# Two groups of 64 rows in place of 65 and 63, and third and fourth pieces stored 16 rows at a time

## The chip, the cores and the metric

The kernel runs on one core of a Trainium2 chip. The metric is device time in microseconds, the median of several executions; the profile is of one further execution. "Span" is the time from the first to the last instruction of that execution.

## What is computed

For each of 16 x 1024 tokens the two largest of 8 router logits are found, the softmax over those two gives two weights, and the token's vector of 512 numbers is written twice, once times each weight (the lower weight first).

```python
batch, seq, hidden, n_experts, k = 16, 1024, 512, 8, 2
topk_indices = np.argsort(probs, axis=-1)[..., -k:]
topk_probs = np.take_along_axis(probs, topk_indices, axis=-1)
topk_probs = topk_probs / np.sum(topk_probs, axis=-1, keepdims=True)
x_expanded = x[:, :, np.newaxis, :].repeat(k, axis=2)
return (x_expanded * topk_probs[..., np.newaxis]).astype(np.float32)
```

All is float32. 33.6 MB of x and 0.5 MB of logits are read, 67.1 MB are written.

## The kernel before

The 16,384 tokens are split over 128 partitions. Every partition has 128 tokens, here called rows: a row of x is 2 KB in a partition, a row of the output 4 KB. The rows are worked on in two groups, of 65 and then 63 rows in a partition (`GROUPS`, line 49). A partition's rows of one group are contiguous in DRAM, so that in the output the blocks of neighbouring partitions begin 260 KB apart in group 0 and 252 KB apart in group 1, and in x 130 and 126 KB.

SBUF holds three tiles: `logits`; `xs`, 65 rows of x (line 95); and `osp`, 16 rows of output (line 96). There is too little room for a group's whole output, which is twice its input, so most of the output is written over rows of x that have been used: `over(r, n, G)` (lines 98 to 104) gives the part of `xs` where the output of rows r to r + n goes.

Group by group, in program order:

1. `LOADS` (lines 51, 111 and 112) loads x in pieces, on SP's queue: 2, 4, 2, 8, 17 and 32 rows in group 0, 16, 16 and 31 in group 1. After the first 6 rows the logits are loaded too (lines 116 and 117), and `top2_weights` computes all weights at once: eleven small VectorE operations and two sigmoids on ScalarE, with a tile for each intermediate result.
2. `plan` (lines 120 to 126) lists the pieces of output. In group 0: rows 0 and 1 into `osp`; rows 2 to 15 into `osp`; rows 16 to 31 over `xs` rows 0 to 31; rows 32 to 39 and 40 to 47 into the two halves of `osp`; rows 48 to 56 over `xs` rows 31 to 48, rows 57 to 64 over 49 to 64. In group 1 rows 0 to 15 are one piece, and the last is rows 48 to 62 (`LAST`, line 54).
3. For each piece VectorE makes one multiply (line 128), then the piece is stored (line 136), on SP's queue except the first piece of 2 rows, which goes on ScalarE's.

Each engine's queue runs in program order. A multiply into `osp` waits for the store that last read that part of `osp`; one over `xs` waits for a store that still reads that part of `xs`. A load of group 1 waits until the stores that read its part of `xs` have landed, and it stands behind all stores of group 0 in SP's queue. The stores of group 1 stand behind its loads.

Of the kernel before, what the change touches and what calls it, by code (L numbers as in the profile page):

```python
# [1 line left out]

# [4 lines left out]

F32 = mybir.dt.float32
ALU = mybir.AluOpType
ACTF = mybir.ActivationFunctionType  # L10
P = 128


def top2_weights(nc, pool, logits, M, E, tag=""):

    hi, lo, n = None, None, E  # L20
    while n > 1:
        n //= 2
        if hi is None:
            a, b = logits[:, :, 0:n], logits[:, :, n : 2 * n]
            nhi = pool.tile([P, M, n], F32, tag=f"hi{n}{tag}")
            nlo = b
            nc.vector.tensor_tensor(nhi, a, b, op=ALU.max)  # L27
            nc.vector.tensor_tensor(nlo, a, b, op=ALU.min)  # L28
        else:
            a, b = hi[:, :, 0:n], hi[:, :, n : 2 * n]  # L30
            nhi = pool.tile([P, M, n], F32, tag=f"hi{n}{tag}")
            nlo = pool.tile([P, M, n], F32, tag=f"lo{n}{tag}")
            tmp = pool.tile([P, M, n], F32, tag=f"tmp{n}{tag}")
            nc.vector.tensor_tensor(tmp, lo[:, :, 0:n], lo[:, :, n : 2 * n], op=ALU.max)  # L34
            nc.vector.tensor_tensor(nlo, a, b, op=ALU.min)  # L35
            nc.vector.tensor_tensor(nlo, nlo, tmp, op=ALU.max)  # L36
            nc.vector.tensor_tensor(nhi, a, b, op=ALU.max)  # L37
        hi, lo = nhi, nlo
    dlt = pool.tile([P, M], F32, tag=f"dlt{tag}")
    nc.vector.tensor_tensor(dlt, hi[:, :, 0], lo[:, :, 0], op=ALU.subtract)  # L40
    WA = pool.tile([P, M, 2], F32, tag=f"WA{tag}")
    nc.scalar.activation(WA[:, :, 0], dlt, ACTF.Sigmoid, scale=-1.0)  # L42
    nc.scalar.activation(WA[:, :, 1], dlt, ACTF.Sigmoid, scale=1.0)  # L43
    return WA

GROUPS = [65, 63]

LOADS = [[2, 4, 2, 8, 17, 32], [16, 16, 31]]


LAST = [[(48, 9), (57, 8)], [(48, 15)]]


@with_exitstack
def kernel(
    ctx: ExitStack,
    tc: tile.TileContext,  # L60
    x: bass.AP,
    router_logits: bass.AP,
    k: bass.AP,
    out: bass.AP,
):
    nc = tc.nc
    B, S, D = x.shape
    E = router_logits.shape[-1]
    N = B * S
    assert int(k) == 2 and E == 8 and N == P * sum(GROUPS)  # L70
    M = N // P

    L = 16
    x_v, o_v, rl_v = [], [], []
    t0 = 0
    for n in GROUPS:
        t1 = t0 + P * n
        x_v.append(
            x.rearrange("b s d -> (b s) d")[t0:t1].rearrange("(p m) d -> p m d", p=P)
        )  # L80
        o_v.append(
            out.rearrange("b s k d -> (b s) k d")[t0:t1].rearrange(
                "(p m) k d -> p m k d", p=P
            )
        )
        rl_v.append(
            router_logits.rearrange("b s e -> (b s) e")[t0:t1].rearrange(
                "(p m) e -> p m e", p=P
            )
        )  # L90
        t0 = t1

    wpool = ctx.enter_context(tc.tile_pool(name="wpool", bufs=1))
    logits = wpool.tile([P, M, E], F32)
    xs = wpool.tile([P, max(GROUPS), D], F32)
    osp = wpool.tile([P, L, 2, D], F32)

    def over(r, n, G):

        a = 2 * r - G
        return xs[:, a : a + 2 * n, :].rearrange("p (r k) d -> p r k d", k=2)

    h = L // 2
    e = 2
    m0 = 0
    for g, G in enumerate(GROUPS):
        r = 0  # L110
        for n in LOADS[g]:
            nc.sync.dma_start(xs[:, r : r + n, :], x_v[g][:, r : r + n, :])  # L112
            r += n
            if g == 0 and r == 6:

                nc.sync.dma_start(logits[:, :G], rl_v[0])  # L116
                nc.sync.dma_start(logits[:, G:], rl_v[1])
                WA = top2_weights(nc, wpool, logits, M, E)
        assert r == G
        begin = [(0, e, osp[:, :e]), (e, L - e, osp[:, e:])] if g == 0 else [(0, L, osp)]  # L120
        plan = begin + [
            (L, L, over(L, L, 2 * L)),
            (2 * L, h, osp[:, :h]),
            (2 * L + h, h, osp[:, h:]),
        ]
        plan += [(r, n, over(r, n, G)) for r, n in LAST[g]]
        for r, n, og in plan:
            nc.vector.tensor_tensor(  # L128
                og,
                xs[:, r : r + n, :].unsqueeze(2).to_broadcast([P, n, 2, D]),  # L130
                WA[:, m0 + r : m0 + r + n, :].unsqueeze(3).to_broadcast([P, n, 2, D]),
                op=ALU.mult,
            )

            queue = nc.scalar if n == e else nc.sync
            queue.dma_start(o_v[g][:, r : r + n], og)  # L136
        m0 += G


# [1 line left out]
_INS = ['x', 'router_logits', 'k']  # L141
_OUTS = [((16, 1024, 2, 512), 'float32')]

_NUMBERS = {'k': 2}


# [26 lines left out]
```

## Time and profile before

| | |
|---|---|
| median of 3 runs | 240.18 us (240.18 to 240.59) |
| the profiled execution's own time | 240.25 us |
| its span | 238.5 us |
| VectorE multiplies into osp | 7, 69.1 us |
| VectorE multiplies over xs | 5, 69.1 us |
| idle time before multiplies into osp | 61.9 us |
| DMA packets | 3312, 101.19 MB, mean 424 GB/s |

The time of a run is 1.8 us longer than the span, for what lies around it. SP's queue has 22 transfers (9 loads of x, 2 of logits, 11 stores), ScalarE's one store. The profile gives for every group of DMA issues the time from issue to landing, so issue plus that time is the moment at which a transfer has landed.

### The profile page before, as it was taken

What the parts mean: (1) busy time and instruction counts of PE and PEld (TensorE: products, weight loads), DVE (VectorE), ACT (ScalarE), POOL (GpSimd) and SP (SyncE); (2) the same over time, 40 slices, a digit from 0 to 9 for tenths busy, and PEclk for the clock granted to TensorE, in tenths of its full rate; (3) what the DMA queues carried; (4) which work ended last, traced back from release to release, by engine and by line L of the source; (5) the groups of instructions that cost most, each with busy time, mean ns of one, the idle gap of its engine ahead of it and who ended that gap; (6) DMA issues with size and microseconds to landing.
All of it is one profiled execution on the core that took longest, in us unless ns stands there. A gap on an engine that the chain in (4) does not pass through costs nothing.

```text
span 238.5 us, 116 instructions
## 1 busy us (share of the span) xinstructions
DVE 142.0 (60%) x23; ACT 1.8 (1%) x3; POOL 0.2 (0%) x4
## 2 busy tenths in 40 slices
DVE  0599999900299699900000699999006999990000
ACT  2000000000000000000000000000000000000000
POOL 0000000000000000000000000000000000000000
DMA  7999989899898999999999999998999989999994
GB/s 261 434 470 411 459 383 528 330 462 462 352 506 352 440 440 440 440 414 465 440 429 434 412 478 458 394 495 374 462 418 429 451 363 429 440 440 429 495 453 206
DMA packets 3312, 101.19 MB, mean 424 GB/s; under 512 B 368, under 2 KB 496, under 8 KB 880
## 3 DMA queue, kind: packets, MB, share of 16 engines
q1 hardware_dynamic: 3168, 100.14, 97.8%
q10 hardware_dynamic: 144, 1.05, 1.0%
HBM read 34.08 MB, written 67.11 MB: 424 GB/s over the span
## 4 chain that ended last, share of the span: by engine, by line
DMA 43%; DVE 41%; issue 4%; SPq 1%; ACT 0%; DVEq 0%
DVE xs L128 22%; DVE osp L128 18%; DMA out_dram<-xs 15%; DMA xs<-in_x_dram 13%; DMA out_dram<-osp 13%; DMA logits<-in_router_logits_dram 3%; SPq L112 0%; DVE nhi L27 0%; DVE logits L28 0%; DVE nlo L36 0%; DVE nhi L37 0%; DVE tmp L34 0%; DVE nlo L35 0%; SPq L116 0%; SPq L136 0%
## 5 line engine op out<-in xcount | busy, mean ns | idle before, releaser
L128 DVE TENSOR_TENSOR osp<-xs,WA 128x8192 f32<-128x8192 f32 (+3 forms) x7 | 69.1, 9908 | 61.9 <-DMA xs<-in_x_dram 31.2
L128 DVE TENSOR_TENSOR xs<-xs,WA 128x16384 f32<-128x16384 f32 (+3 forms) x5 | 69.1, 13812 | 2.2 <-DMA out_dram<-xs 2.0
L27 DVE TENSOR_TENSOR nhi<-logits 128x512 f32<-128x512 f32 x1 | 0.7, 691 | 8.3 <-DMA logits<-in_router_logits_dram 8.3
L42 ACT ACT_TABLE_LOAD x1 | 1.3, 1283 | 0.7 <-PEq L154 0.7
L28 DVE TENSOR_TENSOR logits<-logits 128x512 f32<-128x512 f32 x1 | 0.7, 692 | 0.0
L37 DVE TENSOR_TENSOR nhi<-nhi 128x256 f32<-128x256 f32 (+1 forms) x2 | 0.7, 351 | 0.0
L35 DVE TENSOR_TENSOR nlo<-nhi 128x256 f32<-128x256 f32 (+1 forms) x2 | 0.7, 350 | 0.0
L36 DVE TENSOR_TENSOR nlo<-nlo,tmp 128x256 f32<-128x256 f32 (+1 forms) x2 | 0.7, 350 | 0.0
L34 DVE TENSOR_TENSOR tmp<-logits 128x256 f32<-128x256 f32 x1 | 0.4, 418 | 0.0
L42 ACT ACTIVATE WA<-dlt 128x128 f32<-128x128 f32 x1 | 0.3, 315 | 10.2 <-DVE dlt L40 10.2
L40 DVE TENSOR_TENSOR dlt<-nhi,nlo 128x128 f32<-128x128 f32 x1 | 0.3, 291 | 0.0
L43 ACT ACTIVATE WA<-dlt 128x128 f32<-128x128 f32 x1 | 0.3, 297 | 0.0
L34 DVE TENSOR_TENSOR tmp<-nlo 128x128 f32<-128x128 f32 x1 | 0.3, 283 | 0.0
L154 POOL MEMSET const-bfloat16-1.0<- 128x1 bf16 x1 | 0.1, 101 | 0.0
L154 POOL MEMSET const-uint8-127<- 128x1 uint8 x1 | 0.1, 101 | 0.0
L154 POOL MEMSET const-float32-0.0<- 128x1 f32 x1 | 0.1, 98 | 0.2 <-issue 0.2
L154 POOL MEMSET const-float32-1.0<- 128x1 f32 x1 | 0.1, 98 | 0.0
## 6 DMA issues: line engine op xcount, KB each, us to landing
out_dram<-osp SPq DMA_DIRECT2D x4, 4096.0 KB, 20.7
xs<-in_x_dram SPq DMA_DIRECT2D x2, 4096.0 KB, 29.9
xs<-in_x_dram SPq DMA_DIRECT2D x1, 7936.0 KB, 38.0
out_dram<-xs SPq DMA_DIRECT2D x1, 7680.0 KB, 23.2
out_dram<-osp SPq DMA_DIRECT2D x1, 7168.0 KB, 33.9
out_dram<-xs SPq DMA_DIRECT2D x1, 4608.0 KB, 20.4
xs<-in_x_dram SPq DMA_DIRECT2D x1, 4352.0 KB, 22.4
out_dram<-xs SPq DMA_DIRECT2D x1, 4096.0 KB, 21.5
```

Source lines behind the costliest of these rows:

```text
L27: nc.vector.tensor_tensor(nhi, a, b, op=ALU.max)
L28: nc.vector.tensor_tensor(nlo, a, b, op=ALU.min)
L34: nc.vector.tensor_tensor(tmp, lo[:, :, 0:n], lo[:, :, n : 2 * n], op=ALU.max)
L35: nc.vector.tensor_tensor(nlo, a, b, op=ALU.min)
L36: nc.vector.tensor_tensor(nlo, nlo, tmp, op=ALU.max)
L37: nc.vector.tensor_tensor(nhi, a, b, op=ALU.max)
L40: nc.vector.tensor_tensor(dlt, hi[:, :, 0], lo[:, :, 0], op=ALU.subtract)
L42: nc.scalar.activation(WA[:, :, 0], dlt, ACTF.Sigmoid, scale=-1.0)
L43: nc.scalar.activation(WA[:, :, 1], dlt, ACTF.Sigmoid, scale=1.0)
L128: nc.vector.tensor_tensor(og, xs[:, r : r + n, :].unsqueeze(2).to_broadcast([P, n, 2, D]), WA[:, m0 + r : m0 + r + n, :].unsqueeze(3).to_b ...
L154: nc = _bacc.Bacc("TRN2", target_bir_lowering=False, num_devices=1)
```

## The change

Both groups have 64 rows. In DRAM a partition's block is then 256 KB of output and 128 KB of x in both groups.

`osp` has 18 rows in place of 16. The two more rows (`osp[:, 16:18]`) first hold all intermediate results of `top2_weights`, which had tiles of their own.

The pieces of a group are now written out. The first two (three in group 0) are as before. The third piece, rows 32 to 47, is multiplied in two parts: rows 46 and 47 first, into the two more rows of `osp`, and then rows 32 to 45 into `osp[:, 2:16]`; then one store takes all 16 rows from `osp[:, 2:18]`. The fourth piece, rows 48 to 63, is multiplied in two halves over `xs` rows 32 to 47 and 48 to 63 (`pairs`), and one store takes all 16. The pieces of 17 and 31 rows in `LOADS` become 16 and 32. Group 0 has 5 stores in place of 7 and group 1 has 4 in place of 5.

```diff
-GROUPS = [65, 63]
+GROUPS = [64, 64]
-LOADS = [[2, 4, 2, 8, 17, 32], [16, 16, 31]]
+LOADS = [[2, 4, 2, 8, 16, 32], [16, 16, 32]]
-LAST = [[(48, 9), (57, 8)], [(48, 15)]]
...
-    L = 16
+    L, e = 16, 2
...
-    osp = wpool.tile([P, L, 2, D], F32)
+    osp = wpool.tile([P, L + e, 2, D], F32)
-    def over(r, n, G):
-        a = 2 * r - G
+    def pairs(a, n):
         return xs[:, a : a + 2 * n, :].rearrange("p (r k) d -> p r k d", k=2)
...
+    def multiply(og, m0, r, n):
+        nc.vector.tensor_tensor(
+            og,
+            xs[:, r : r + n, :].unsqueeze(2).to_broadcast([P, n, 2, D]),
+            WA[:, m0 + r : m0 + r + n, :].unsqueeze(3).to_broadcast([P, n, 2, D]),
+            op=ALU.mult,
+        )
...
+                spare = osp[:, L:].rearrange("p r k d -> p (r k d)")
+                WA = top2_weights(nc, wpool, logits, spare, M, E)
...
+        if g == 0:
+            multiply(osp[:, :e], m0, 0, e)
+            nc.scalar.dma_start(o_v[g][:, :e], osp[:, :e])
+            multiply(osp[:, e:L], m0, e, L - e)
+            nc.sync.dma_start(o_v[g][:, e:L], osp[:, e:L])
+        else:
+            multiply(osp[:, :L], m0, 0, L)
+            nc.sync.dma_start(o_v[g][:, :L], osp[:, :L])
+
+        multiply(pairs(0, L), m0, L, L)
+        nc.sync.dma_start(o_v[g][:, L : 2 * L], pairs(0, L))
+
+        multiply(osp[:, L:], m0, 3 * L - e, e)
+        multiply(osp[:, e:L], m0, 2 * L, L - e)
+        nc.sync.dma_start(o_v[g][:, 2 * L : 3 * L], osp[:, e:])
+
+        multiply(pairs(2 * L, L // 2), m0, 3 * L, L // 2)
+        multiply(pairs(3 * L, L // 2), m0, 3 * L + L // 2, L // 2)
+        nc.sync.dma_start(o_v[g][:, 3 * L :], pairs(2 * L, L))
```

In `top2_weights` the tiles of the intermediate results are taken from that spare part one after another (`part(n)`); its operations and their order are the same.

More of the change, by code (lines that the diff above doesn't have):

```diff
@@ L11, with top2_weights, part @@
 P = 128
-def top2_weights(nc, pool, logits, M, E, tag=""):
+def top2_weights(nc, pool, logits, scratch, M, E):
+    at = 0
+    def part(n):
+        nonlocal at
+        at += M * n
+        return scratch[:, at - M * n : at].rearrange("p (m n) -> p m n", n=n)
     hi, lo, n = None, None, E
@@ L22, in top2_weights @@
         n //= 2
+        nhi = part(n)
         if hi is None:
             a, b = logits[:, :, 0:n], logits[:, :, n : 2 * n]
-            nhi = pool.tile([P, M, n], F32, tag=f"hi{n}{tag}")
             nlo = b
@@ L30, in top2_weights @@
             a, b = hi[:, :, 0:n], hi[:, :, n : 2 * n]
-            nhi = pool.tile([P, M, n], F32, tag=f"hi{n}{tag}")
-            nlo = pool.tile([P, M, n], F32, tag=f"lo{n}{tag}")
-            tmp = pool.tile([P, M, n], F32, tag=f"tmp{n}{tag}")
+            nlo, tmp = part(n), part(n)
             nc.vector.tensor_tensor(tmp, lo[:, :, 0:n], lo[:, :, n : 2 * n], op=ALU.max)
@@ L38, in top2_weights @@
         hi, lo = nhi, nlo
-    dlt = pool.tile([P, M], F32, tag=f"dlt{tag}")
+    dlt = part(1)[:, :, 0]
     nc.vector.tensor_tensor(dlt, hi[:, :, 0], lo[:, :, 0], op=ALU.subtract)
-    WA = pool.tile([P, M, 2], F32, tag=f"WA{tag}")
+    WA = pool.tile([P, M, 2], F32)
     nc.scalar.activation(WA[:, :, 0], dlt, ACTF.Sigmoid, scale=-1.0)
@@ L95 @@
     xs = wpool.tile([P, max(GROUPS), D], F32)
-    osp = wpool.tile([P, L, 2, D], F32)
-    def over(r, n, G):
-        a = 2 * r - G
+    osp = wpool.tile([P, L + e, 2, D], F32)
+    def pairs(a, n):
         return xs[:, a : a + 2 * n, :].rearrange("p (r k) d -> p r k d", k=2)
-    h = L // 2
-    e = 2
+    def multiply(og, m0, r, n):
[5 more added lines that the diff above has]
+        )
     m0 = 0
@@ L117 @@
                 nc.sync.dma_start(logits[:, G:], rl_v[1])
-                WA = top2_weights(nc, wpool, logits, M, E)
+                spare = osp[:, L:].rearrange("p r k d -> p (r k d)")
+                WA = top2_weights(nc, wpool, logits, spare, M, E)
         assert r == G
[L120 to L136, printed above, removed]
+        if g == 0:
[14 more added lines that the diff above has]
+        nc.sync.dma_start(o_v[g][:, 3 * L :], pairs(2 * L, L))
         m0 += G
```

## The prediction

> **What bounds the kernel now.** I read the totals and the rows of the DMA queues first, then the waits, then the timeline with the time to landing of the single stores.
>
> ```profile
> span 238.5 us, 116 instructions
> DVE 142.0 (60%) x23; ACT 1.8 (1%) x3; POOL 0.2 (0%) x4
> q1 hardware_dynamic: 3168, 100.14, 97.8%
> q10 hardware_dynamic: 144, 1.05, 1.0%
> HBM read 34.08 MB, written 67.11 MB: 424 GB/s over the span
> ```
>
> VectorE works 60% of the time. The packets of the two DMA queues (q1 is SP's, q10 ScalarE's) fill 98.8% of what 16 DMA engines have in the span. So the path that sets the end is the DMA engines' own work, and what VectorE waits for matters only if it leaves them without a transfer. Whether it does is seen by setting each transfer's issue beside the landing of the transfer ahead of it. For the last stores:
>
> ```profile
> 180.91 17.29 DVE L128 TENSOR_TENSOR osp<-xs,WA 128x8192 f32<-128x8192 f32 x2 [13.39 <-DMA out_dram<-osp]
> 189.63 8.93 SPq L136 DMA_DIRECT2D out_dram<-osp  x2
> 198.24 16.16 DVE L128 TENSOR_TENSOR xs<-xs,WA 128x15360 f32<-128x15360 f32 x1
> 214.42 0.33 SPq L136 DMA_DIRECT2D out_dram<-xs  x1
> ```
>
> The answers for the windows in which 150.28, 167.54, 189.63, 198.23 and 214.42 lie give the time from issue to landing:
>
> ```profile
> out_dram<-osp SPq DMA_DIRECT2D x1, 30.5
> out_dram<-xs SPq DMA_DIRECT2D x1, 32.6
> out_dram<-osp SPq DMA_DIRECT2D x1, 4096.0 KB, 20.2
> out_dram<-osp SPq DMA_DIRECT2D x1, 4096.0 KB, 21.3
> out_dram<-xs SPq DMA_DIRECT2D x1, 7680.0 KB, 23.2
> ```
>
> They land at 180.8, 200.1, 209.8, 219.5 and 237.6 us. The steps between the landings are 19.3 us (16 rows), 9.7 and 9.7 (8 rows each) and 18.1 (15 rows): 1.209 us for every row of a store, whatever the store's size, and nothing between them. A row is 512 KB over the 128 partitions; a row of a load, half as many bytes, is worth 0.604. Each was issued before the one ahead had landed; the smallest lead is 219.5 - 214.4 = 5.1 us. By this price the whole kernel (128 rows loaded, 128 stored, 512 KB of logits) is 128 x 0.604 + 128 x 1.209 + 1.2 = 233.3 us of queue, out of 237.6 to the last landing. The other 4.3 us lie at the start (about 2.6: the 8-row load, the fourth of x, lands at 14.4 us with 10.9 us of bytes in, the rest being issue and first latency; it does not change), in the stretch from there to 47.0 (0.6), and in the changes of direction between loads and stores.
>
> **The change, part by part.**
>
> *Bytes and packets.* The same rows are loaded and stored. In place of seven stores of 8, 8, 9, 8 and 8, 8, 15 rows there are four of 16: three fewer, 64 rows to 64 rows. Saved per pair by the steps above: 9.7 + 9.7 - 19.3 = 0.1 us at the rounding of the rows, under 0.05 by the landings' second decimals; for three about -0.1. The load of 17 rows becomes 16 and the one of 31 becomes 32: 0.6 us out and 0.6 us in, sum 0. The Trainium skill ("SBUF — State Buffer", The DMA setup-cost knee) puts roughly 2 us on every transfer and asks for the largest single one; by that page three fewer would be worth an estimated 6 us. Here the measured step from one landing to the next shows no such cost, because a transfer's fixed part runs under the one ahead of it.
>
> *VectorE.* 2 + 14 rows in place of 8 + 8: 2.29 + 15.09 against 2 x 8.69, both seen in the trace, 17.4 each. The last pieces become 8 + 8 rows. Scratch for the top-2 step moves into the two spare rows: the same eleven small operations, 1,792 of 2,048 numbers. The first multiply into them must follow ScalarE's read of dlt (ended at 12.7) and comes after 47 us. Cost 0, and VectorE is hidden by the queue as long as its stores are issued in time.
>
> *The removed wait.* With 65 rows the 9-row piece is written from row 31 of xs, which the store of rows 0 to 31 still reads. With 64 it starts at row 32:
>
> ```profile
> DVE xs L128 <- DMA out_dram<-xs: 2.0, 1, 2.0
> DVE osp L128 <- DMA out_dram<-osp: 30.1, 2, 16.7
> ```
>
> The 2.0 us go, but behind them stood a store that would queue anyway: 0. The 30.1 us (the output buffer read by its store) stay; the two rows multiplied early, 2.3 us each time, fall into them.
>
> *What is late next: the leads.* This is the part that could cost. I follow the new order with the same durations. Group 0: the 32-row load lands at 46.4 (0.6 earlier, a row less ahead of it), the 14-row store at 63.3, the store of rows 16 to 31 at 82.7. VectorE multiplies rows 46 and 47 at 47.3 to 49.6, waits for 63.3, then needs 15.1 where before 8.7 were enough for a store: issue at 78.5 (before: 72.7). The queue has work until 82.7, so the lead is 4.2 us (before 10.5). The next 17.4 us of multiplying end at 95.9, with work until 102.0: lead 6.1. The loads of group 1 stand behind that store in SP's queue. The first two, which wait only for the store that landed at 82.7, follow at 96.3 and 96.7 (before 102.3 and 113.5); the third waits for xs rows 32 to 63 to be stored, 121.4 (before 123.5), with queue until 140.7. Queued behind it on SP is only the first store of group 1, whose data are ready at about 148.4. Group 1 repeats it: the piece of 2 + 14 rows waits for the store landing at 179.4, is issued at 194.6 with work until 198.7 (lead 4.2), the last store is issued at 212.0 with work until 218.1 (lead 6.1) and lands 19.3 later, 237.4. How long a store needs from issue to first byte is not shown alone. From below it is 0; from above, the first load (issued at 0.73 into an empty queue) takes 3.65 us to its landing, 1.2 of it bytes, so 2.4. I take that upper value, the nearest row: still inside the lead of 4.2. Cost 0, with 4.2 - 2.4 = 1.8 us to spare.
>
> *Pitch.* In DRAM one partition's block is 64 x 4 KB = 256 KB for the output and 128 KB for x, where it was 260 and 252, 130 and 126. No row of this trace shows a pitch that is a power of two, so the cost is bounded. From below: 0, since 260 and 252 KB run at the same 1.209 us a row; a gain is excluded to the extent that the packets run at one rate already. From above, by the nearest stretch in which transfers hold one another up: from 14.4 to 47.0 us, 49 load rows and the 2 rows of ScalarE's store should take 49 x 0.604 + 2 x 1.209 = 32.0 and take 32.6, 1.9% more. On all 128 store rows that is 154.8 x 0.019 = +2.9 us. I take 0, by the nearest rows in kind: the packets of two different pitches with no difference. The Trainium skill ("DMA: Bandwidth & Descriptors", Latency and other measured facts) speaks against the change here: copies with a power-of-two row pitch slow down, 207 GB/s at 512 KiB where a padded pitch gave 214, half of that at 4 MiB. By the 512 KiB figure the stores would lose an estimated 3%, about 5 us; 256 KiB is below its table and no run shows it yet.
>
> *Sum.* 237.6 - 0.1 (stores) - 0.1 (the smaller first load's share and rounding) = 237.4 to the last landing. The profiled execution took 240.25 with a span of 238.5, so 240.0 to 240.1 for this one; its own time is 0.07 above the median of the runs, 240.18. I predict **240.0 us**. No change here means within 0.2%, 239.7 to 240.7, about what a measurement of this kernel can tell from nothing.
>
> **The rivals.**
>
> *Pitch (slower).* The stores of both groups run at a lower rate because 16 engines stand 256 KB apart. For it: the row stride is the only property of the transfers that changes everywhere, and the queue has no idle share to absorb it. Against it: the rows of before show one rate for all. It decides from 0.3% of the 154.8 us of stores on (0.5 us); at its upper bound of 1.9% the time is 243.0.
>
> *A hole in the queue (slower).* The lead of 4.2 us at 78.5 and 194.6 is shorter than any before. If a store needed more than that from issue to first byte, each microsecond would be paid twice: 240.0 + 2 x 1 = 242 at 5.2 us. Against it: the 2.4 us bound, and the 5.1 us lead of before left no gap.
>
> *Boundaries vanish (faster).* Fewer, equal transfers could also remove the 0.6 us between 14.4 and 47.0 and the 0.2 at the store-to-load turn: 240.0 - 0.8 = 239.2. Against it: the same loads and the same turns of direction remain.
>
> *That it does not do what it says*: the two early rows would have to wait for the output buffer's store and not overlap it; then 2.3 us go on both leads of 4.2, leaving 1.9, and the time is the hole's: at worst 0.5 us twice, 241.0. It is counted with the hole.
>
> **How the numbers follow.** Forecast 0.48; pitch 0.33; the hole 0.04; boundaries 0.15. Faster by over 0.2% is the boundaries' 0.15; slower is 0.33 + 0.04 = 0.37; within is 0.48. The forecast's own range is 239.7 to 240.6. The range that holds 8 in 10 goes down to 239.3 (most of the boundaries) and up to pitch's bound, 243.0.
>
> **What would show it.** Forecast: landings of 16-row stores 19.3 us apart, the last near 237.4, issue leads of 4.2 and 6.1. Pitch: the same leads or longer, but steps of 19.4 to 19.7, in both groups, and shares over 98% with lower GB/s. Hole: a step of over 19.3 exactly at the third store of a group (issued near 78.5 or 194.6) and a lower share of q1. Boundaries: the 32-row load landing near 45.8. I am wrong if the store steps are off 19.3 by more than 0.1.

## The result, and the profile after

| | before | after |
|---|---|---|
| median of 22 runs, us | 240.19 | 240.9 |
| lowest and highest, us | 240.08, 241.08 | 240.39, 242.5 |
| the profiled execution, us | 240.25 | 241.28 |
| its span, us | 238.5 | 239.5 |

The changed kernel is slower: the ratio is 1.0031, with a 95% interval of 1.0018 to 1.0044. The forecast was 240.0 us and no change, with a range of its own of 239.7 to 240.6. The runs of after are also more scattered: its lowest lies 0.3 us above the lowest of before, its highest 1.4 us above the highest. The profiled execution of after lies 0.4 us above its median, so what it shows is somewhat too large.

The totals of its page, in the order of before:

```profile
span 239.5 us, 109 instructions
DVE 142.2 (59%) x24; ACT 1.8 (1%) x3; POOL 0.2 (0%) x4
q1 hardware_dynamic: 2736, 100.14, 97.5%
q10 hardware_dynamic: 144, 1.05, 1.0%
HBM read 34.08 MB, written 67.11 MB: 422 GB/s over the span
```

The same bytes in 432 packets fewer, VectorE's work as before, the queues still 98.5% full. Then the last stores of the timeline (start, length, instruction, idle time before it):

```profile
180.54 15.09 DVE L99 TENSOR_TENSOR osp<-xs,WA 128x14336 f32<-128x14336 f32 x1 [12.10 <-DMA out_dram<-osp]
195.66 0.33 SPq L135 DMA_DIRECT2D out_dram<-osp  x1
195.66 17.42 DVE L99 TENSOR_TENSOR xs<-xs,WA 128x8192 f32<-128x8192 f32 x2
213.11 0.33 SPq L140 DMA_DIRECT2D out_dram<-xs  x1
```

and the time from issue to landing of the four stores of group 1, issued at 149.01, 166.26, 195.66 and 213.11:

```profile
out_dram<-osp SPq DMA_DIRECT2D x1, 31.5
out_dram<-xs SPq DMA_DIRECT2D x1, 33.6
out_dram<-osp SPq DMA_DIRECT2D x1, 23.5
out_dram<-xs SPq DMA_DIRECT2D x1, 25.3
```

They land at 180.5, 199.8, 219.1 and 238.4: 19.3 us apart, the step of before for 16 rows. The shortest leads are 199.82 - 195.66 = 4.2 us here and 82.95 - 78.78 = 4.2 in group 0, and no gap follows. So neither the rate of the stores nor a hole in the queue (the DMA engines left without a transfer) is where the time went. VectorE's waits:

```profile
DVE osp L99 <- DMA xs<-in_x_dram: 35.5, 1, 35.5
DVE osp L99 <- DMA out_dram<-osp: 26.5, 2, 14.4
```

The 2.0 us for the store from xs are gone, and the 30.1 us for osp have become 26.5, since two rows are multiplied meanwhile. Neither counts: the queue was never short of work.

**Where it went.** I split the time between landings of both traces into stretches, and take from each what its bytes cost at 0.6045 us a load row (19.345 us for 16 stored rows, about the step of before, and the same for 32 loaded). What is left is time lost there. "Loads, group 0" goes from the landing of the 8-row load to that of the 14-row store; "stores to loads" from the landing of the second piece's store to that of group 1's second load; "loads to stores" from there to the landing of group 1's first store; "last stores" from there to the last landing; "closing" from there to the end of the span.

```
                     before   after   difference
8-row load lands at   14.36   14.11     -0.25
loads, group 0         0.61    1.16     +0.55
stores to loads        0.10    0.40     +0.30
loads to stores        0.11    0.44     +0.33
last stores           -0.04   -0.10     -0.06
closing                0.87    1.05     +0.18
```

The first two rows come from these transfers, issued at 3.36 and 30.07 before,

```profile
xs<-in_x_dram SPq DMA_DIRECT2D x1, 2048.0 KB, 11.0
out_dram<-osp SPq DMA_DIRECT2D x1, 7168.0 KB, 33.9
```

and at 3.08 and 29.86 after:

```profile
xs<-in_x_dram SPq DMA_DIRECT2D x1, 2048.0 KB, 11.0
out_dram<-osp SPq DMA_DIRECT2D x1, 7168.0 KB, 33.8
```

Between the two landings lie 49.6 us before and 49.5 after, but after has a load row less to move. With -0.01 in the store of the second piece the differences add up to 1.04, the two spans' difference of 1.03. The start lies within the scatter of the profiles (14.1 to 14.65 us in all kernels with that load). The stores gain 0.06, as forecast. All losses lie where reads from DRAM and writes to it follow one another or overlap, and at the very end.

**The end** can be read from SP's instructions on the launch line, before first and after second (number, shortest, median and longest ns, first and last start):

```profile
L168 SPq EVENT_SEMAPHORE  x7: 17/27/28, 214.8 to 238.4; - x7
```

```profile
L172 SPq EVENT_SEMAPHORE  x7: 17/27/28, 238.5 to 239.4; - x7
```

At the end SP waits for the semaphores of all transfers, five waits in a fixed order, about 62 ns from one to the next (238.466, 238.519, 238.581, 238.645, 238.707 in after's trace). The transfers share eight semaphores, and which one the last transfer has depends on how many there are. The last of 23 transfers has one that is waited for fourth, so that this wait and one more end behind its landing at 237.60; the last of 20 has the one waited for first, so that all five end behind the landing at 238.45. The two other instructions of the seven belong to the final barrier.

**The turn from stores to loads.** Before, the last two stores of group 0 were issued at 93.15 and 101.87 and the second load of group 1 at 113.52:

```profile
out_dram<-xs SPq DMA_DIRECT2D x1, 4608.0 KB, 20.4
out_dram<-xs SPq DMA_DIRECT2D x1, 4096.0 KB, 21.5
xs<-in_x_dram SPq DMA_DIRECT2D x1, 4096.0 KB, 29.1
```

From the landing of the first, 113.5, to that of the load, 142.6, it takes 29.1 us, where the bytes (8 stored and 32 loaded rows) cost 29.0. After, by time to landing of the last two stores of group 0 (issued at 78.78 and 96.23) and of the second load of group 1 (issued at 97.36):

```profile
out_dram<-osp SPq DMA_DIRECT2D x1, 23.5
out_dram<-xs SPq DMA_DIRECT2D x1, 25.8
xs<-in_x_dram SPq DMA_DIRECT2D x1, 4096.0 KB, 44.0
```

They land at 102.3, 122.0 and 141.4. The store of 16 rows that has the loads behind it takes 19.7 us in place of 19.3, and these loads give nothing back: 39.1 us from 102.3 to 141.4 for 38.7 of bytes.

### The profile page after: what moved, and what is told of

Its sections match the earlier page's. It is cut to its first block, busy times and chain, and to the rows that moved or that the text cites. A ratio compares the mean times of both kernels' runs of the same rounds, so it can differ in the third digit from the quotient of the medians.

```text
span 239.5 us, 109 instructions
## 1 busy us (share of the span) xinstructions
DVE 142.2 (59%) x24; ACT 1.8 (1%) x3; POOL 0.2 (0%) x4
## 3 DMA queue, kind: packets, MB, share of 16 engines
q10 hardware_dynamic: 144, 1.05, 1.0%
## 4 chain that ended last, share of the span: by engine, by line
DMA 44%; DVE 43%; SPq 1%; issue 1%; ACT 0%; DVEq 0%
DMA out_dram<-osp 27%; DVE osp L99 27%; DMA xs<-in_x_dram 15%; DVE xs L99 15%; DMA logits<-in_router_logits_dram 2%; SPq L110 0%; DVE osp L29 0%; DVE logits L30 0%; DVE osp L36 0%; DVE osp L37 0%; DVE osp L35 0%; DVE osp L34 0%; SPq L114 0%; SPq L140 0%; ACT WA L42 0%
## 5 line engine op out<-in xcount | busy, mean ns | idle before, releaser
L99 DVE TENSOR_TENSOR osp<-xs,WA 128x2048 f32<-128x2048 f32 (+2 forms) x7 | 69.3, 9908 | 62.6 <-DMA xs<-in_x_dram 35.5
L99 DVE TENSOR_TENSOR xs<-xs,WA 128x8192 f32<-128x8192 f32 (+1 forms) x6 | 69.2, 11536 | 0.2
L29 DVE TENSOR_TENSOR osp<-logits 128x512 f32<-128x512 f32 x1 | 0.7, 692 | 8.1 <-DMA logits<-in_router_logits_dram 8.1
L35 DVE TENSOR_TENSOR osp<-osp 128x256 f32<-128x256 f32 (+1 forms) x2 | 0.7, 352 | 0.0
L37 DVE TENSOR_TENSOR osp<-osp 128x256 f32<-128x256 f32 (+1 forms) x2 | 0.7, 352 | 0.0
L36 DVE TENSOR_TENSOR osp<-osp 128x256 f32<-128x256 f32 (+1 forms) x2 | 0.7, 352 | 0.0
L42 ACT ACTIVATE WA<-osp 128x128 f32<-128x128 f32 x1 | 0.3, 315 | 10.0 <-DVE osp L40 10.0
L40 DVE TENSOR_TENSOR osp<-osp 128x128 f32<-128x128 f32 x1 | 0.3, 293 | 0.0
L43 ACT ACTIVATE WA<-osp 128x128 f32<-128x128 f32 x1 | 0.3, 298 | 0.0
L34 DVE TENSOR_TENSOR osp<-osp 128x128 f32<-128x128 f32 x1 | 0.3, 285 | 0.0
```

Source lines behind the costliest of these rows:

```text
L99: nc.vector.tensor_tensor(og, xs[:, r : r + n, :].unsqueeze(2).to_broadcast([P, n, 2, D]), WA[:, m0 + r : m0 + r + n, :].unsqueeze(3).to_b ...
```

## The experiments

Each was timed in 8 to 12 runs beside 21 to 35 of the kernel before on the same chip; ratios have their 95% interval. The first two theories were the pitch in DRAM and the merged stores.

**Groups of 64 rows, stores still in halves**

```diff
-GROUPS = [65, 63]
+GROUPS = [64, 64]
-LOADS = [[2, 4, 2, 8, 17, 32], [16, 16, 31]]
+LOADS = [[2, 4, 2, 8, 16, 32], [16, 16, 32]]
-LAST = [[(48, 9), (57, 8)], [(48, 15)]]
+LAST = [[(48, 8), (56, 8)], [(48, 16)]]
```

> The kernel before with groups of 64 and 64 rows, its stores still in halves (8 + 8). If the pitch of 256 and 128 KB in DRAM is the cause, this already has the loss: ratio to before 1.002 to 1.004, with the steps of the 32-row load of group 1 near 19.8 us and the turn from stores to loads near 19.7 in place of 19.3. If the cause is the merged 16-row stores, it stays at 0.999 to 1.001 and those steps are those of before (about 19.4).

1.0022 (1.0006 to 1.0038), 240.68 us. The loss is there without any merged store of osp, as the theory of the pitch says.

**The changed kernel with a pitch of 65 rows**

```diff
-            x.rearrange("b s d -> (b s) d")[t0:t1].rearrange("(p m) d -> p m d", p=P)
+            x.rearrange("b s d -> (b s) d")[: P * 65].rearrange(
+                "(p m) d -> p m d", p=P
+            )[:, :n]
```

and the same for the output.

> The changed kernel, but both groups read and write the first 65 x 128 tokens with a pitch of 65 rows (260 and 130 KB), 64 of 65 rows used; the rest of the output is not written. Bytes, packets and order are those of the changed kernel. If pitch is the cause: ratio to before 0.999 to 1.001. If the merged stores are: 1.002 to 1.004, as the changed kernel.

1.0021 (1.0004 to 1.0037), 240.74 us: the pitch alone doesn't bring the time back. But its turn from stores to loads is clean. The stores were issued at 78.89 and 96.35, the load at 97.48:

```profile
out_dram<-osp SPq DMA_DIRECT2D x1, 23.5
out_dram<-xs SPq DMA_DIRECT2D x1, 25.4
xs<-in_x_dram SPq DMA_DIRECT2D x1, 4096.0 KB, 43.6
```

Landings at 102.4, 121.7 and 141.1, 38.7 us from the first to the last, which is its bytes.

**Its control, pitch 64 on one region** (65 replaced by 64 in that edit)

> The control of the run with a pitch of 65: both groups on the first 64 x 128 tokens with a pitch of 64 rows (256 and 128 KB); the rest of the output is not written. Both theories: as the changed kernel, ratio 1.002 to 1.004. If it is nearer 1.000, reading and writing the same half twice matters, and the run with pitch 65 says nothing.

1.0015 (0.9999 to 1.0031), 240.81 us; its median is that of the changed kernel in the next run, and the turn costs 0.24.

**The changed kernel again**

> The changed kernel once more on the same chip, as the mark for the others: ratio to before 1.002 to 1.004, single runs spread over about 2 us where those of before lie within 0.5. In its profile the excess should again lie at the turns from loads to stores and from stores to loads, not in the stretches of stores alone.

1.0019 (1.0007 to 1.0031), 240.80 us. Its profiled execution was its shortest (240.32) and lost only 0.71, 0.29 and 0.03 in the three places: single profiles scatter by as much as the effect, and only the turn from stores to loads was steady.

By the times neither theory held alone, so I tried what all four slower kernels share.

**The kernel before with a 16-row load beside ScalarE's store**

```diff
-LOADS = [[2, 4, 2, 8, 17, 32], [16, 16, 31]]
+LOADS = [[2, 4, 2, 9, 16, 32], [16, 16, 31]]
```

> The kernel before (65 and 63 rows, stores in halves) with one load changed: group 0 loads 2, 4, 2, 9, 16, 32 rows, so that the load that shares the DMA engines with ScalarE's store has 16 rows and 32 KB packets, as in all four slower runs, in place of 17 rows and 34 KB. Theory A (that load is slowed more by the store beside it): ratio to before 1.001 to 1.002, packets of 32 KB between 16 and 24 us up to 0.3 us longer. Theory B (the load of 32 rows ahead of the turn to stores in group 1): 1.000, since that load still has 31 rows. Theory C (16-row tiles and places in SBUF that the group sizes set): 1.000.

1.0001 (0.999 to 1.0012), 240.27 us.

**The changed kernel with the 17-row load**

```diff
-LOADS = [[2, 4, 2, 8, 16, 32], [16, 16, 32]]
+LOADS = [[2, 4, 2, 8, 17, 31], [16, 16, 32]]
```

> The changed kernel with group 0 loading 2, 4, 2, 8, 17, 31 rows: the load beside ScalarE's store has 17 rows again, as before. Theory A: ratio to before falls from 1.002 to about 1.000 or 1.001. Theories B and C: it stays at 1.002.

1.0019 (1.0009 to 1.0028), 240.74 us. By their times both speak against theory A. Their packets don't quite: between 12 and 37 us, where the load runs beside ScalarE's store, those of an engine together took 0.29 us longer than packets of their size elsewhere in the kernel before with the 16-row load (0.16 and 0.22 in the two profiles of before) and 0.26 here (0.43 and 0.34 in those of the changed kernel).

**The changed kernel with 16-row loads ahead of group 1's turn**

```diff
-LOADS = [[2, 4, 2, 8, 16, 32], [16, 16, 32]]
+LOADS = [[2, 4, 2, 8, 16, 32], [16, 16, 16, 16]]
```

> The changed kernel with group 1 loading 16, 16, 16, 16 rows: the load ahead of the turn to stores has 16 rows and 32 KB packets in place of 64 KB. Theory B: the packets ahead of the turn are stretched less, ratio to before 1.000 to 1.001, and the step from the third load's start to the end of loads near 19.4 us in place of 19.4 to 20.3. Theories A and C: 1.002.

1.0012 (1.0002 to 1.0023), 240.62 us, with 0.28 us still lost at that turn, which speaks against theory B. Its 21 transfers leave four closing waits behind the landing, and the closing took 1.00 us; that number led to the theory on the end.

**The kernel before, against itself**

> The kernel before, against itself: ratio 0.999 to 1.001, which says how much of 0.2% the measurement can tell. Its profile is a second sample of the three places where the changed kernel lost time: excess of the packets between 16 and 24 us (0.17 us an engine in the first profile), the turn from stores to loads (0.06) and the turn from loads to stores near 158 us (0.09). Theories A and B each need theirs to stay clearly below the changed kernel's.

0.9994 (0.9985 to 1.0002). The three places lost 0.61, 0.14 and 0.18 us, near the first profile of before.

**Tile of 65 rows, and the rest of the grid.** The edit of `xs` below, in the changed kernel, in the one with pitch 65 and in the one with split stores; and the split stores with pitch 65 and no such edit:

```diff
-    xs = wpool.tile([P, max(GROUPS), D], F32)
+    xs = wpool.tile([P, max(GROUPS) + 1, D], F32)
```

> The changed kernel with the tile xs one row longer (65 rows, the last never used), so that osp lies 130 KB behind the start of xs in SBUF as before, not 128 KB. Theory D (the places in SBUF: loads into xs and stores from osp meet at a power of two): ratio to before falls from 1.002 to 1.000. Theory E (the pitch in DRAM and the merged stores each cost about 0.2% and do not add): stays at 1.002. Theory F (pitch in DRAM alone): 1.002.

1.0034 (1.0024 to 1.0044).

> The changed kernel with a pitch of 65 rows in DRAM (both groups on the first 65 x 128 tokens, 64 of 65 rows used, the rest of the output not written) and the tile xs one row longer. Theory D: 1.000. Theory E: 1.002, the merged stores are left. Theory F: 1.000, but then the run with pitch 65 and the shorter tile should have been 1.000 too, and it was 1.0021.

1.0020 (1.0009 to 1.0030).

> Groups of 64 rows, stores in halves, pitch 64 in DRAM, xs one row longer. Theory D: 1.000. Theories E and F: 1.002.

1.0008 (0.9999 to 1.0016).

> Groups of 64 rows with the stores in halves as before, a pitch of 65 rows in DRAM (both groups on the first 65 x 128 tokens, the rest of the output not written), xs of 64 rows. Theory D: 1.002, since osp still lies 128 KB behind xs. Theories E and F: 1.000; the turn from stores to loads should cost 0.0 to 0.1 us, as in both other kernels with an odd pitch, where a pitch of 64 cost 0.24 to 0.41.

1.0024 (1.0008 to 1.004), runs from 240.07 to 242.15.

Theory D falls with the first two, F with the second and the last, E with the last, where both wanted 1.000. The turn of the last, 0.16, is above the 0.0 to 0.1 that was expected and below every profile with a pitch of 64. No cell of the grid has the time of the kernel before for certain; split stores with the longer tile come nearest, and their interval meets that of the split stores without it. What was left were the end, and groups of other heights.

**The changed kernel with 23 transfers**

```diff
-LOADS = [[2, 4, 2, 8, 16, 32], [16, 16, 32]]
+LOADS = [[2, 4, 2, 8, 16, 16, 16], [16, 16, 16, 8, 8]]
```

> The changed kernel with three loads cut in two or three (group 0 loads 2, 4, 2, 8, 16, 16, 16 rows, group 1 loads 16, 16, 16, 8, 8), so that it has 23 transfers as the kernel before and the last store signals a semaphore that SP waits for late. Theory G (part of the loss is SP's closing waits, some 62 ns each, five behind the last landing and two before): from the last landing to the end 0.87 us in place of 1.05, the rest unchanged, ratio lower by 0.0008. Theory H (all of the loss is in the DMA engines' work): ratio as the changed kernel, 1.002 to 1.003.

1.0006 (0.9990 to 1.0021), 240.36 us; the interval is too wide to tell 0.0008 from nothing. The closing went as theory G said, 237.49 to 238.36 = 0.87 us:

```profile
L172 SPq EVENT_SEMAPHORE  x7: 17/27/28, 212.6 to 238.3; - x7
```

The first wait is over at 212.6, long before the last landing. "The rest unchanged" was wrong: the cut loads also lost only 0.53 us in group 0. The turn from stores to loads, which the cuts do not touch, still cost 0.35.

**Merged stores with groups of 65 and 63 rows** (the changed kernel; its loads and last pieces as in `LOADS` and `LAST` of before)

```diff
-GROUPS = [64, 64]
+GROUPS = [65, 63]
-LOADS = [[2, 4, 2, 8, 16, 32], [16, 16, 32]]
+LOADS = [[2, 4, 2, 8, 17, 32], [16, 16, 31]]
+LAST = [[(48, 9), (57, 8)], [(48, 15)]]
...
-        multiply(pairs(2 * L, L // 2), m0, 3 * L, L // 2)
-        multiply(pairs(3 * L, L // 2), m0, 3 * L + L // 2, L // 2)
-        nc.sync.dma_start(o_v[g][:, 3 * L :], pairs(2 * L, L))
+        for r, n in LAST[g]:
+            multiply(pairs(2 * r - G, n), m0, r, n)
+            nc.sync.dma_start(o_v[g][:, r : r + n], pairs(2 * r - G, n))
```

> The changed kernel's first three pieces (16-row stores, 18 rows of osp, two multiplied early) with the groups of 65 and 63 rows and the last pieces of before. If groups of 64 rows are what is slow: 1.000 and 0.0005 for four closing waits. If merged stores slow the turns: 1.002.

1.0010 (1.0001 to 1.0020), 240.49 us, between the two expectations. 21 transfers, closing 1.00 us; the turn from stores to loads 0.13.

**Groups of 66 and 62 rows** (the kernel before, scratch in two rows of `osp`, `LAST` of 9, 9 and 14 rows)

```diff
-GROUPS = [65, 63]
+GROUPS = [66, 62]
-LOADS = [[2, 4, 2, 8, 17, 32], [16, 16, 31]]
+LOADS = [[2, 4, 2, 8, 18, 32], [16, 16, 30]]
```

> The kernel before with groups of 66 and 62 rows (264 and 248 KB apart in DRAM; 18 rows in the fifth load, 30 in the last), its scratch in two rows of osp. If 64 rows are special: 1.000. If the kernel before is fast by its odd 65 and 63 alone: 1.001 to 1.002.

1.0001 (0.9991 to 1.0011), 240.15 us: scratch inside `osp` costs nothing, and 65 and 63 are not alone in being fast.

**Groups of 63 and then 65 rows** (the kernel before, its `LAST` exchanged too)

```diff
-GROUPS = [65, 63]
+GROUPS = [63, 65]
-LOADS = [[2, 4, 2, 8, 17, 32], [16, 16, 31]]
+LOADS = [[2, 4, 2, 8, 16, 31], [17, 16, 32]]
```

> The kernel before with its groups exchanged, 63 rows first and 65 then, so that the last load has 32 rows. If the 31-row last load is what makes the kernel before fast: 1.001 to 1.002, with the turn from loads to stores in group 1 near 0.3 us over its bytes in place of 0.11 to 0.18. If 64 rows are what is slow: 1.000.

1.0008 (1.0000 to 1.0017), 240.31 us. The turn from loads to stores lost nothing behind a 32-row load, so it is not its load of 31 rows that makes the kernel before fast.

**The load at the first turn cut in two**, in the kernel before and in the one with 66 and 62 rows:

```diff
-LOADS = [[2, 4, 2, 8, 17, 32], [16, 16, 31]]
+LOADS = [[2, 4, 2, 8, 17, 16, 16], [16, 16, 31]]
```

> The kernel before with its 32-row load in group 0 cut into 16 and 16, 24 transfers in all. If the stretch of the last packets goes with their size: from the landing of the 8-row load to that of the 14-row store 0.3 to 0.5 us less than before (0.61 over its bytes), and SP's closing 0.06 us shorter: ratio 0.998 to 0.999, 239.7 to 239.9 us. If the cut kernel's short stretch was chance: 1.000.

1.0002 (0.9991 to 1.0012), 240.24 us against 240.31.

> The kernel with groups of 66 and 62 rows (ratio 1.0001 uncut) with the same cut, 24 transfers. Packet size: 0.998 to 0.999. Chance: 1.000.

1.0004 (0.9995 to 1.0013), 240.26 us. In both profiles the stretch lost less, 0.35 and 0.38 us, and the closing took 0.81 with 24 transfers, but the times don't show it. No version beats the kernel before by more than the measurement tells.

**All runs together.** By the times, the twelve measurements of kernels with two groups of 64 rows have ratios of 1.0006 to 1.0034, the seven of other heights 0.9994 to 1.0010. What the stretches cost, in us over the bytes, one profile each:

```
                      groups of 64 rows                          other heights
stores to loads       pitch 64: 0.40 0.26 0.24 0.29 0.26         0.10 0.14 0.14 0.13
                        0.26 0.34 0.24 0.35                      0.12 0.05 0.13 0.17
                      pitch 65: -0.01 0.13 0.16
loads, group 0        pitch 64: 1.16 0.81 1.21 0.71 0.81         0.61 0.61 0.76
  (load not cut)        0.82 1.11 1.10                           0.79 0.80 0.76
                      pitch 65: 1.10 1.19 1.00
loads to stores       pitch 64: 0.44 0.14 0.92 0.03 0.23         0.11 0.18 0.18 0.27
                        0.28 0.17 0.36 0.18                      0.02 0.00 0.13 0.08
                      pitch 65: 0.33 0.24 0.56
closing               20 transfers 1.05, 21 1.00, 23 0.87, 24 0.81
```

## Why the prediction was wrong

**What held.** The DMA engines' work set the end in both kernels. Issues were where the prediction put them until the losses moved them: 78.78 and 96.23 in group 0 (78.5 and 95.9 forecast), the shortest leads 4.2 us in both groups with no gap, the last stores 0.06 us cheaper. The removed wait and the early rows were worth nothing. The rivals of the hole and of the vanishing boundaries are out. All steps from one 16-row store to the next are 19.3 us but one: the last store of group 0, at the turn, took 19.7, which is over the 0.1 that the prediction named as the sign of being wrong.

**What failed** is the sum, at two of its terms; for the rest of the loss the runs show no cause.

*"237.4 to the last landing ... so 240.0 to 240.1"* took what lies behind the last landing as before. Fewer transfers gave the last store a semaphore that SP waits for first, and five waits in place of two stand behind it. That is +0.18 us, shown in the traces: 1.05 us in all kernels with 20 transfers, 1.00 with 21, 0.87 with 23, whether the stores are in halves or merged (the version with cut loads), 0.81 with 24. The order of SP's closing waits stood in before's trace; the prediction has no term for it.

*"Pitch ... I take 0"* and *"the same turns of direction remain"*: the pitch was priced on the stores' rate and the changes of direction were taken as constants. The stores' rate does not depend on the pitch, so the rival as I wrote it (steps of 19.4 to 19.7 in both groups) fell too. But the one turn from stores to loads costs 0.24 to 0.40 us with a pitch of 64 rows in all nine profiles, and -0.01 to 0.17 in eleven with another: 0.29 against 0.11 on the mean, +0.18. The packets say the same: between 94 and 150 us those of an engine together took 0.06 to 0.23 us longer than packets of their size elsewhere in the nine, -0.01 to 0.04 in the eleven. The run with pitch 65 and its control differ in nothing else. So for the turn the pitch is shown to be the cause, though not by what mechanism. The rule of the Trainium skill that the prediction weighed ("DMA: Bandwidth & Descriptors", Latency and other measured facts) is for copies from DRAM to DRAM; here a power of two showed only at that turn, and the estimate of 5 us on all stores was far too high.

The prediction also has a slip in its account of before: the start is 14.4 - 10.9 = 3.5 us, not 2.6. Nothing rests on it, since the start was held constant.

*What stays open.* The other stretches with loads lost more on the mean with two groups of 64 rows: in group 0 1.00 against 0.72 us (11 and 6 profiles, uncut loads), at the turn to stores 0.32 against 0.12 (12 and 8). With 0.18 for the turn from stores to loads, 0.18 for closing and -0.06 for the last stores this makes 0.28 + 0.20 + 0.18 + 0.18 - 0.06 = 0.78 us, where the medians differ by 0.71. But these 0.48 us are means of scattered values, and they do not follow the pitch (the three profiles with 65 lost as much), nor the merged stores, the places in SBUF or, by the times, the size of a single load. In group 0 the loss comes and goes: four of the eleven profiles lost 0.71 to 0.82, hardly more than other heights, and seven 1.00 to 1.21, and these seven are the ones whose profiled execution took 240.89 us or more. The packets narrow the place: those ahead of the first store (41 to 49 us) were stretched as much with other heights (0.61 us an engine on the mean, 0.54 with 64 rows), while those beside ScalarE's store (12 to 37 us) were stretched by 0.16 to 0.34 with other heights and 0.26 to 0.51 with 64 rows. Why two groups of 64 rows should lose this I can't say; the cause stays open.

## What to carry to other kernels

Where the DMA queue is full, a step between two landings is the price of a transfer: set it against bytes, stretch by stretch, and the loss shows, here where reads and writes of DRAM meet, and not in the totals. Here the bytes were the same and the queue stayed full, and what the change moved lay at the boundaries and the end. Price these one by one, with the waits behind the last landing, of which more or fewer are left depending on how many transfers there are. A difference of 0.3% needs many runs and several profiles.

## What the runs showed of the hardware

- Where group 0's last load is followed by stores, its last packets are stretched: in after's trace the last 64 KB packet of each of the 16 engines ahead of 46.7 us took 2.8 to 3.2 us, not the 2.42 of the others, while the first packets of the store behind it took their usual time. Before's trace has the same there, 2.9 to 3.2 us, so this is a price of the turn and not of the change. 32 KB packets at the same place were stretched by 0.14 us an engine in the cut version of the changed kernel, and by 0.25 in that of the kernel before. At the turn to stores in group 1 (150 to 164 us) the stretch went from nothing to 0.39 us an engine.
- Two stores of 8 rows cost 9.67 + 9.68 us, one of 16 rows 19.3: with a full queue the size of a transfer did not matter from 4 to 8 MB. Stores of 9 and 15 rows took 10.9 and 18.1 us, in proportion.
- A store with a lead of 4.2 us over the end of the queue left no gap.
